# Gate projections of a hybrid decoder layer, done in pairs by seven half-size products

## The chip, the cores and the metric

The kernel runs on one core of a Trainium2 chip. The metric is device time in microseconds (us); smaller is better. Times are those of whole executions, with a profile of one execution beside them. Engines: TensorE (PE, matmul), VectorE (DVE), ScalarE (ACT), GpSimd (POOL) and SyncE (SP, which issues most DMAs).

## The reference

One layer in float32, 512 tokens of 2048 channels. The input is RMS-normalised and projected by `w_in`; one branch is a gated linear recurrence (HGRN2, 8 heads), the other sparse attention (NSA, 16 heads in 4 groups: compressed, selected and window keys). Both go through an output matrix, are merged by sigmoid gates, and go through `w_out` with a residual and a last norm. What matters here:

```
xn = rmsnorm(h, norm_w[layer])
proj = xn @ w_in[layer]                      # 2048 x 15408, the last 4096 columns are merge_g
o_hg = hgrn2_chunkwise(...) ; y_hg = o_hg @ w_branch_hg[layer]
o_nsa = nsa_attention(...) * silu(nsa_z)     # nsa_z: 2048 columns of proj
y_nsa = o_nsa @ w_branch_nsa[layer]
g_hg, g_nsa = split(sigmoid(merge_g))
h = h + (g_hg * y_hg + g_nsa * y_nsa) @ w_out[layer]
return rmsnorm(h, final_norm_w)
```

## The kernel before

All products are done in float32r with both operands split in a high and a low part: high x high, high x low, low x high (`mm3`, L133 to L136). The weights come from HBM in units of 512 KB (`load_w`, L111): SP issues the load into one of three buffers `wr`, ACT casts it to the high part `wh` (L125), DVE subtracts to get the low part `wl` (L126); `wh` and `wl` have two buffers each. `split` (L129) does the same for other tiles. A projection of 128 columns (`proj_units`, L138) takes two units and 16 steps, one per row block; a step is three matmuls of 512 columns (all tokens). It gives back control after each step, so that `weave` (L170) can lay the steps of another generator between them, with two numbers that say how many steps each has.

The stages, in order: the ramp (L190: normalise, transpose x to `xh` and `xl`, first values and branch gates, token tile by token tile); HGRN2 (L305: `hg_proj` of the next head woven with `hg_core` of this one; every second `hg_proj` also does a pair of values by `proj_v`, 64 steps of three 256-column matmuls); NSA compression (L497); the four NSA groups (L566: `nsa_proj` of the next group woven with `nsa_core`, 220 steps against 48); the branch outputs and merge (L745); the output projection (L776).

The 32 gate tiles (`merge_gates`, L159: a projection, Sigmoid on ACT, a DMA by POOL to `gat_d` in DRAM) are filler. Three lie beside the last HGRN2 core (L474), 16 in the compression (L509), 8 beside the last NSA core (L741), 5 in the wait for the branch inputs (L748). The 16 z tiles are in `nsa_proj` (`z_proj`, L586), 64 of its 220 steps; they are multiplied into the attention output at L723 and L734. The HGRN2 branch output is computed in the last loop (L767) beside the NSA one.

The framework sets each engine's order by priorities, in general that of the code; `tc.high_priority()` puts a unit's split ahead.

Of the kernel before, what the change touches and what calls it, by code (L numbers as in the profile page):

```python
# [8 lines left out]
F32 = mybir.dt.float32  # L9
# [9 lines left out]
KD = D // P  # L19
HG = 8  # L20
# [25 lines left out]
def constants():  # L46
    """Tables that depend on shapes alone: identity, causal masks, RoPE angles, block masks."""
# [27 lines left out]
def body(tc, a, out):  # L75
# [33 lines left out]
    gat_d = dram.tile([2, KD, P, S], F32, name="gat_d")  # L109

    def load_w(src, k0, nk, *cols, raw=None, hi=None, lo=None, urgent=True):  # L111
        """A unit of weights (nk row blocks, the given column ranges) and its exact split in two float32r parts."""
# [25 lines left out]
    def proj_units(acc, src, c0, ncol, xh, xl, nk):  # L138
        """acc[ncol, tokens] = src[:, c0:c0+ncol]^T x, in steps of one row block."""
# [7 lines left out]
    def proj_v(vb, cols):  # L147
        """vb[i // 2][tokens, i % 2, 256 columns] = x w_in[:, cols], two token tiles to a bank."""
# [17 lines left out]

    def proj_t(*args):
# [15 lines left out]
    xh = xpool.tile([P, KD, S], F32R, name="xh")  # L183
    xl = xpool.tile([P, KD, S], F32R, name="xl")
# [5 lines left out]
    with pool("st_a") as sp:  # L190
        xt = [sp.tile([P, D], F32, name="xt", bufs=4) for _ in range(4)]
# [14 lines left out]
        # the activation table and the tensor engine's clock are up by the time the data arrives  # L206
# [98 lines left out]
    with pool("hg") as hp:  # L305
        hgw = sv[:, R_HGW:R_HGW + 1]
        heads = {}
        vts = {0: vt}
# [3 lines left out]
        def hg_proj(head):  # L312
            pr, e = divmod(head, 2)
            if pr and not e:
                vb = [bank() for _ in range(2)]
                yield from proj_v(vb, ((C_HI + pr * 256, 256),))
                v = vts[pr] = vpool.tile([P, 4, 2, P], F32, name="vt", bufs=2)
                for n in range(2):
                    nc.scalar.copy(v[:, 2 * n:2 * n + 2].rearrange("p j e c -> p (j e c)"), vb[n])
# [15 lines left out]
        def hg_core(head):  # L335
# [136 lines left out]
        for head in range(HG - 1):  # L472
            weave(hg_proj(head + 1), 112 if head % 2 else 48, hg_core(head), 17)
# [23 lines left out]
    with pool("cp") as cp:  # L497
# [14 lines left out]
        for b, (w1, w2, pos0, b0) in enumerate(((a["cmp_k_w1"], a["cmp_k_w2"], R_KP, R_KB),  # L512
# [5 lines left out]
            for l0 in range(0, CLEN, 8):  # L518
# [344 lines left out]
```

## Time and profile before

| | us |
|---|---|
| three executions | 2112.49, 2110.85, 2112.24 (median 2112.24) |
| span of the profiled execution | 2108.8 |
| PE, DVE, ACT, POOL busy in it | 2085.3, 998.1, 746.6, 310.6 |

Of the profiled execution the span is given, from the first to the last instruction; what lies around it is not in it. Busy times of PE are modelled: a matmul's duration contains its way through the array, which overlaps with the next, so the time that a matmul costs is read from how many start in a stretch. In the views a line is that of the code, tiles are written out<-in, and `[... <-X]` tells what ended the idle time ahead of an instruction.

### The profile page before, as it was taken

Reading aid. Unit: us, or ns where it says so; the run is one execution under the profiler, and the core shown is the slowest. Engines: PE = TensorE matmul, PEld = TensorE weight load, DVE = VectorE, ACT = ScalarE, POOL = GpSimd, SP = SyncE. Lnnn points to the kernel's source line nnn. Section 1 sums busy time; section 2 is a strip of 40 time slices with the busy share of each in tenths; the row PEclk is TensorE's granted clock in tenths of the full one; section 3 lists DMA queues with packets and bytes.
Section 4 is the critical chain, followed back from the end, with each engine's and each line's share of the span. In section 5 each row is a group of like instructions: output and inputs, shape, how many; then the busy total and the mean of one; then the engine's idle time right before and its main releaser. Section 6 shows DMA issues by size and latency. Waiting matters only on the chain.

```text
span 2108.8 us, 26626 instructions
## 1 busy us (share of the span) xinstructions
PE 2085.3 (99%) x10560; PEld 1761.7 (84%) x10560; DVE 998.1 (47%) x1595; ACT 746.6 (35%) x1149; POOL 310.6 (15%) x367
## 2 busy tenths in 40 slices
PE   8999999999999999999999999999999999999998
PEld 7888888888888888889889888888888888888887
DVE  7364636365544432435545555555553433433343
ACT  4223232333233433225344444434553322222232
POOL 2131414132000000101311221121220000000000
PEclk9999999999999999999999999999999999999999
DMA  6223222234355554332222232223225744445232
GB/s 184 61 85 86 83 82 80 81 85 115 100 158 171 171 171 120 100 96 70 77 81 81 78 84 80 75 74 89 79 83 169 209 130 123 127 133 201 95 132 88
DMA packets 328641, 231.38 MB, mean 110 GB/s; under 512 B 9931, under 2 KB 298516, under 8 KB 327876
## 3 DMA queue, kind: packets, MB, share of 16 engines
q1 hardware_dynamic: 316388, 198.36, 32.5%
q10 hardware_dynamic: 7552, 16.57, 2.1%
q0 software_dynamic: 4576, 14.75, 2.1%
q8 instruction: 83, 1.36, 0.3%
q14 instruction: 42, 0.34, 0.1%
HBM read 210.71 MB, written 18.94 MB: 109 GB/s over the span
## 4 chain that ended last, share of the span: by engine, by line
PE 93%; DVE 3%; issue 2%; POOL 1%; ACT 1%; DMA 0%; SPq 0%; DVEq 0%; POOLq 0%; ACTq 0%
PE pj L134 23%; PE pj L136 23%; PE pj L135 23%; PE sc L135 4%; PE sc L134 4%; PE sc L136 4%; PE pt L708 2%; PE po L134 2%; PE po L135 2%; PE po L136 2%; DVE wl L126 1%; PE pt L396 1%; PE pt L136 1%; PE pt L134 1%; PE pt L135 1%
## 5 line engine op out<-in xcount | busy, mean ns | idle before, releaser
L126 DVE TENSOR_TENSOR wl<-wr,wh 128x1024 fp32r<-128x1024 f32 x308 | 382.1, 1241 | 609.4 <-ACT wh L125 606.2
L134 PE MATMUL pj<-xh,wh 128*128 128x512 f32 x1664 | 659.0, 396 | 0.0
L136 PE MATMUL pj<-xh,wl 128*128 128x512 f32 x1664 | 651.7, 392 | 0.4 <-DVE wl L126 0.4
L135 PE MATMUL pj<-xl,wh 128*128 128x512 f32 x1664 | 649.2, 390 | 0.0
L125 ACT CAST wh<-wr 128x1024 fp32r<-128x1024 f32 x308 | 323.5, 1051 | 845.6 <-PE pj L135 610.6
L136 PEld LDWEIGHTS pj<-xh,wl 128*128 128x128 f32 x1664 | 312.4, 188 | 68.0 <-DVE wl L126 1.2
L134 PEld LDWEIGHTS pj<-xh,wh 128*128 128x128 f32 x1664 | 312.7, 188 | 61.3 <-DVE vl L131 0.6
L135 PEld LDWEIGHTS pj<-xl,wh 128*128 128x128 f32 x1664 | 312.8, 188 | 60.4
L134 PE MATMUL pj<-wh,xh 128*128 128x256 f32 (+1 forms) x544 | 167.0, 307 | 0.0
L136 PE MATMUL pj<-wh,xl 128*128 128x256 f32 (+1 forms) x544 | 164.0, 301 | 0.0
L135 PE MATMUL pj<-wl,xh 128*128 128x256 f32 (+1 forms) x544 | 163.9, 301 | 0.0
L689 POOL TENSOR_SCALAR s<-s,sm 128x512 f32<-128x512 f32 (+3 forms) x128 | 87.7, 697 | 192.8 <-DVE sm L687 112.8
L135 PEld LDWEIGHTS pj<-wl,xh 128*128 128x128 f32 x544 | 103.6, 190 | 4.7
L134 PEld LDWEIGHTS pj<-wh,xh 128*128 128x128 f32 x544 | 103.5, 190 | 4.8
L136 PEld LDWEIGHTS pj<-wh,xl 128*128 128x128 f32 x544 | 103.5, 190 | 3.8
L134 PE MATMUL pj<-onh,wh 128*128 128x512 f32 x256 | 99.6, 389 | 0.0
L135 PE MATMUL pj<-onl,wh 128*128 128x512 f32 x256 | 99.6, 389 | 0.0
L136 PE MATMUL pj<-onh,wl 128*128 128x512 f32 x256 | 99.6, 389 | 0.0
L684 ACT ACTIVATE s<-s,mx 128x512 f32<-128x512 f32 (+3 forms) x128 | 70.9, 555 | 58.7 <-DVE mx L682 57.6
L131 DVE TENSOR_TENSOR ptl<-pt,pth 128x512 fp32r<-128x512 f32 (+1 forms) x80 | 50.7, 634 | 77.1 <-ACT pth L130 77.0
L493 POOL TENSOR_TENSOR rsh<-rsh,rope 32x512 f32<-32x512 f32 x28 | 45.5, 1626 | 240.5 <-DVE rsh L492 224.6
L361 POOL TENSOR_TENSOR suf<-suf,pre 128x256 f32<-128x256 f32 x56 | 57.3, 1022 | 124.1 <-DVE pre L344 105.1
(316 smaller groups left out, 2715.4 us busy)
## 6 DMA issues: line engine op xcount, KB each, us to landing
wr<-in_w_in_dram SPq DMA_DIRECT2D x220, 512.0 KB, 3.7
wr<-in_w_branch_nsa_dram SPq DMA_DIRECT2D x32, 512.0 KB, 3.9
wr<-in_w_out_dram SPq DMA_DIRECT2D x32, 512.0 KB, 3.7
wr<-in_cmp_k_w_dram SPq DMA_DIRECT2D x16, 512.0 KB, 3.5
wr<-in_cmp_v_w_dram SPq DMA_DIRECT2D x16, 512.0 KB, 3.6
wr<-in_w_in_dram SPq DMA_DIRECT2D x32, 256.0 KB, 3.4
gg<-gat_d ACTq DMA_DIRECT2D x16, 512.0 KB, 4.3
wr<-in_w_branch_hg_dram SPq DMA_DIRECT2D x16, 512.0 KB
```

The lines of the kernel that those rows point to most:

```text
L125: nc.scalar.copy(hi[:, :n], raw[:, :n])
L126: nc.vector.tensor_tensor(lo[:, :n], raw[:, :n], hi[:, :n].bitcast(F32), op=OP.subtract)
L131: nc.vector.tensor_tensor(lo, src, hi.bitcast(F32), op=OP.subtract)
L134: nc.tensor.matmul(acc, lhsT=lh, rhs=rh, start=start, stop=False, **kw)
L135: nc.tensor.matmul(acc, lhsT=lh, rhs=rl, start=False, stop=False, **kw)
L136: nc.tensor.matmul(acc, lhsT=ll, rhs=rh, start=False, stop=stop, **kw)
L361: nc.gpsimd.tensor_tensor(fv[:, :, 0], fv[:, :, 0], whole(pv[:, :, 1]), op=OP.mult)
L396: nc.tensor.matmul(pv[:, j].rearrange("p (m h) -> p m h", h=h), lhsT=qk[:, j * P:(j + 1) * P], rhs=up, start=True, stop=True)
L493: nc.gpsimd.tensor_tensor(sh, sh, sin, op=OP.mult)
L684: nc.scalar.activation(s[:, b], s[:, b], AF.Exp, scale=SCALE, bias=mx[:, b:b + 1], accum_out=sm[:, b:b + 1])
L689: nc.gpsimd.tensor_scalar(s[:, b], s[:, b], sm[:, b:b + 1], 1.0, op0=OP.mult, op1=OP.mult)
L708: nc.tensor.transpose(ps[:, o:o + P], sc[i][:, b, j * P:(j + 1) * P], ident)
```

## The change

Twenty-six of the 32 gate tiles are computed between the ramp and HGRN2, in 13 pairs. A pair is a product of 256 columns of `w_in`, 2048 rows and 512 tokens; each of the three is halved, and in place of eight products of halves there are seven, with sums of halves of x (made once, `sums`, with 64 transposes) and sums of halves of the weights (made on DVE for every pair). A half-size product (`product`) has eight row blocks: the high weights are loaded and 512 columns stream by (256 tokens of the high and 256 of the low part of x), then the low weights with the 256 columns of the high part. The two halves of a bank are added later on DVE.

The values of the second pair of heads are done with `sums`, ahead of the pairs; the z tiles and the HGRN2 branch output become filler (`z_units`, `y_hg`, through `z_d` and `part_d` in DRAM), six gate tiles stay as filler ahead of the branch stage, and z is multiplied in when the attention output is read back.

```diff
+NG = 26
+    def z_units(n0, n1, pl, tag="mg"):
+        for n in range(n0, n1):
+            acc = bank()
+            yield from proj_units(acc, w_in, C_Z + n * DH, DH, xh, xl, KD)
+            st = pl.tile([P, S], F32, name=tag, bufs=2)
+            nc.scalar.activation(st, acc, AF.Sigmoid)
+            nc.vector.tensor_tensor(st, acc, st, op=OP.mult)
+            nc.gpsimd.dma_start(z_d[n], st)
+    def sevens(src, c_lo, c_hi, kh, side, chain, keeps, done):
...
+        def load(r, c0, dst=None):
+            if dst is None:
+                dst = wp.tile([P, 1024], F32, name="wr", bufs=3)
+            nc.sync.dma_start(v(dst), block(r, c0))
+            return dst
+        def add(dst, r, c0):
+            more = load(r, c0)
+            with tc.high_priority():
+                nc.vector.tensor_tensor(dst[:, :kh * P], dst[:, :kh * P], more[:, :kh * P], op=OP.add)
+        def parts(raw):
+            hi, lo = (wp.tile([P, 1024], F32R, name=n, bufs=2) for n in ("wh", "wl"))
+            with tc.high_priority():
+                split(hi[:, :kh * P], lo[:, :kh * P], raw[:, :kh * P])
+            return v(hi), v(lo)
+        def product(acc, p, w, first):
+            av = acc.rearrange("p (b t) -> p b t", b=2)
+            for k in range(kh):
+                x = side(p, k)
+                nc.tensor.matmul(av, lhsT=w[0][:, k], rhs=x, start=first and k == 0, stop=False, skip_group_check=True)
+                nc.tensor.matmul(av[:, 0], lhsT=w[1][:, k], rhs=x[:, 0], start=False, stop=k == kh - 1,
+                                 skip_group_check=True)
...
+        load(0, c_lo, X)
+        A = bank()
+        w = parts(X)
+        add(X, 0, c_hi)
+        load(0, c_hi, Y)
+        yield from product(A, 0, w, True)
+        nc.scalar.copy(s1, A)
+        B = bank()
+        w = parts(X)
+        add(Y, 1, c_hi)
+        add(X, 1, c_hi)
+        yield from product(B, 1, w, True)
+        nc.scalar.copy(s5, B)
+        b22 = load(1, c_hi)
+        w, w2 = parts(X), parts(b22)
+        add(X, 1, c_lo)
+        yield from product(A, 2, w, False)
+        nc.scalar.copy(s2, A)
+        yield from product(B, 3, w2, False)
+        nc.vector.tensor_tensor(s2, B, s2, op=OP.add)
+        yield from product(A, 4, parts(Y), False)
+        nc.vector.tensor_tensor(s5, A, s5, op=OP.add)
+        b21 = load(1, c_lo)
+        B = bank()
+        yield from product(B, 5, parts(b21), True)
+        nc.vector.tensor_tensor(s2[:, :h], s2[:, :h], s2[:, h:], op=OP.add)
+        nc.vector.tensor_tensor(s2[:, h:], s5[:, :h], s5[:, h:], op=OP.add)
+        nc.vector.tensor_tensor(s1, B, s1, op=OP.add)
+        nc.vector.tensor_tensor(s1[:, :h], s1[:, :h], s1[:, h:], op=OP.add)
+        yield from product(A, 6, parts(X), False)
+        nc.scalar.copy(s5[:, :h], A[:, h:])
+        nc.vector.tensor_tensor(s1[:, h:], A[:, :h], s5[:, :h], op=OP.add)
+        done(s1, s2)
...
+        def sums():
...
+            for n, (i0, c0) in enumerate(((2, H), (0, 0), (0, H), (2, 0))):
+                for t in range(2):
+                    for k0 in (0, 4):
+                        ps = lbank().rearrange("p (k t) -> p k t", k=4)
+                        for k in range(4):
+                            c = c0 + (k0 + k) * P
+                            nc.tensor.transpose(ps[:, k], xt[i0 + t][:, c:c + P], ident)
+                        ts = slice(t * P, (t + 1) * P)
+                        split(sx[:, 0, n, k0:k0 + 4, ts], sx[:, 1, n, k0:k0 + 4, ts], ps)
+                        yield
+        weave(values(1), 64, sums(), 16)
...
+            def gates(lo, hi):
+                for o, v, sign in ((0, lo, 1.0), (1, hi, -1.0)):
+                    nc.scalar.activation(v, v, AF.Sigmoid, scale=sign)
+                    nc.gpsimd.dma_start(gat_d[(n + o) // KD, (n + o) % KD], v)
...
-            weave(hg_proj(head + 1), 112 if head % 2 else 48, hg_core(head), 17)
-        weave(merge_gates(0, 3, hp), 48, hg_core(HG - 1), 17)
+            weave(hg_proj(head + 1), 112 if head in (3, 5) else 48, hg_core(head), 17)
+        weave(z_units(0, 3, hp), 48, hg_core(HG - 1), 17)
...
-        fill = merge_gates(3, 19, cp)
+        def y_hg():
+            for c in range(KD):
+                acc = bank()
+                yield from proj_units(acc, a["w_branch_hg"], c * P, P, og[0], og[1], HG)
+                g = cp.tile([P, S], F32, name="mg", bufs=2)
+                nc.scalar.dma_start(g, gat_d[0, c])
+                nc.vector.tensor_tensor(g, acc, g, op=OP.mult)
+                nc.gpsimd.dma_start(part_d[c], g)
+        def both():
+            yield from z_units(3, 8, cp)
+            yield from y_hg()
+        fill = both()
...
-                    for _ in range(8):
+                    for _ in range(6 + l // 2 % 2):
...
-        weave(nsa_proj(g + 1), 220, nsa_core(g), 48)
-    weave(merge_gates(19, 27, ap, "raw"), 112, nsa_core(GROUPS - 1), 48)
+        weave(nsa_proj(g + 1), 156, nsa_core(g), 48)
+    weave(z_units(8, 16, ap, "raw"), 112, nsa_core(GROUPS - 1), 48)
...
-        fill = merge_gates(27, 32, bp)
+        fill = merge_gates(NG, 32, bp)
```

Behind the ramp DVE's row before is that of HGRN2's first heads: splits of weight units (`wl`), with the core's work behind them.

```order
L126 TENSOR_TENSOR wl<-wr,wh 128x1024 x4
L332 TENSOR_TENSOR zs<-pj,zs 128x512
L126 TENSOR_TENSOR wl<-wr,wh 128x1024 x2
L342 TENSOR_SCALAR kt<-sg,nomlb,omlb 128x512
L344 TENSOR_SCALAR pre<-sg,omlb,lbt 128x512
```

Now one pair stands there 13 times. Below is DVE from the first split of a pair (its first buffer is `xt_2155`, the next pair's is `xt_2333`, loaded operands are `wr`, `xt_908` and `s2` hold results; L134 is a split, L203 an add of weights).

```order
L134 TENSOR_TENSOR wl_2160<-xt_2155,wh_2159 128x1024
L203 TENSOR_TENSOR xt_2155<-xt_2155,wr_2163 128x1024
L252 TENSOR_TENSOR xt_908<-pj_1980,xt_908 128x256
L134 TENSOR_TENSOR wl_2186<-xt_2155,wh_2185 128x1024
L203 TENSOR_TENSOR xt_2155<-xt_2155,wr_2192 128x1024
L134 TENSOR_TENSOR wl_2215<-xt_2155,wh_2214 128x1024
L203 TENSOR_TENSOR xt_2155<-xt_2155,wr_2222 128x1024
L134 TENSOR_TENSOR wl_2219<-wr_2212,wh_2218 128x1024
L134 TENSOR_TENSOR wl_2260<-xt_2155,wh_2259 128x1024
L240 TENSOR_TENSOR s2_2156<-pj_2184,s2_2156 128x512
L203 TENSOR_TENSOR xt_2333<-xt_2333,wr_2367 128x1024
L134 TENSOR_TENSOR wl_2284<-wr_2280,wh_2283 128x1024
```

Between two splits of the same buffer stands the add that changes it; the split of the sixth product (the last row) stands behind a sum that reads the fourth product's bank and behind the first add of the next pair.

On ACT the row before, in HGRN2, is casts of weight units (`wh`) between the core's copies and activations.

```order
L125 CAST wh<-wr 128x1024
L330 ACTIVATE zs<-pj 128x512
L432 COPY kn<-pt 128x384
L441 COPY st<-sc 128x128
L455 ACTIVATE ob<-po 128x512
```

Now ACT has this across the end of a pair (`xt_2333` is the pair's first buffer, `xt_2511` that of the next; L451 is a gate's Sigmoid).

```order
L133 CAST wh_2461<-wr_2458 128x1024
L133 CAST wh_2485<-xt_2333 128x1024
L451 ACTIVATE s2_2334<-s2_2334 128x512
L133 CAST wh_2515<-xt_2511 128x1024
L251 COPY xt_908<-pj_2336 128x256
L133 CAST wh_2541<-xt_2511 128x1024
```

The Sigmoid of a gate stands ahead of the first cast of the next pair, and a copy out of the seventh product's bank ahead of the second.

SP issues the eight loads of a pair in one row. Six of them share the three buffers `wr`, so each waits until DVE has done with an earlier one: the load for the first add of the next pair waits for the third add of this one, and the load behind it, for the add to `Y` of the next pair, for the split of the fourth product.

## Rows read from the trace of the kernel before

**Rows 1.** The page: busy time of the engines, and the chain that ended last.
```profile
PE 2085.3 (99%) x10560; PEld 1761.7 (84%) x10560; DVE 998.1 (47%) x1595; ACT 746.6 (35%) x1149; POOL 310.6 (15%) x367
...
PE 93%; DVE 3%; issue 2%; POOL 1%; ACT 1%; DMA 0%; SPq 0%; DVEq 0%; POOLq 0%; ACTq 0%
```

**Rows 2.** Busy time in stretches of the span (first row: the columns).
```profile
core 0: us, PE busy (x) PEld busy (x) DVE busy (x) ACT busy (x) POOL busy (x), PEclk, DMA share, GB/s
0.00:61.00 61.00, 51.19 (x286) 45.30 (x287) 40.35 (x65) 28.48 (x47) 13.99 (x14) 0.92 0.52 159
61.00:503.00 442.00, 438.13 (x2562) 374.81 (x2561) 229.30 (x318) 133.30 (x182) 126.63 (x137) 1.00 0.29 82
503.00:819.00 316.00, 315.55 (x1407) 259.41 (x1407) 137.29 (x120) 116.64 (x134) 16.64 (x22) 1.00 0.53 154
820.00:839.00 19.00, 19.00 (x161) 19.00 (x160) 3.68 (x3) 3.14 (x3) 0.58 (x1) 1.00 0.29 78
...
1481.00:1592.00 111.00, 110.58 (x554) 92.09 (x553) 58.77 (x163) 61.98 (x124) 24.58 (x41) 1.00 0.28 79
1592.00:1700.00 108.00, 108.00 (x477) 89.03 (x476) 45.61 (x43) 37.49 (x42) 5.07 (x9) 1.00 0.62 187
1700.00:1850.00 150.00, 150.00 (x663) 124.23 (x662) 57.99 (x65) 35.13 (x37) 0.00 (x0) 1.00 0.44 133
```

**Rows 3.** Waits of PE over the span: total us, times, longest us.
```profile
PE sc L396 <- DVE ad L400: 3.9, 7, 0.8
...
PE pj L136 <- DVE wl L126: 0.4, 1, 0.4
PE po L134 <- ACT pch L130: 0.4, 1, 0.4
```

**Rows 4.** Groups by line and shape: count | busy us, mean ns | idle before.
```profile
L126 DVE TENSOR_TENSOR wl<-wr,wh 128x1024 fp32r<-128x1024 f32 x308 | 382.1, 1241 | 609.4 <-ACT wh L125 606.2 <-DMA wr<-in_w_in_dram 3.0
L125 ACT CAST wh<-wr 128x1024 fp32r<-128x1024 f32 x308 | 323.5, 1051 | 845.6 <-PE pj L135 610.6 <-PE pj L136 68.0 <-PE po L136 51.7
...
L362 DVE TENSOR_TENSOR pre<-pre 128x256 f32<-128x256 f32 x56 | 26.7, 477 | 15.5 <-POOL suf L361 15.2
...
L164 ACT ACTIVATE mg<-pj 128x512 f32<-128x512 f32 x24 | 14.2, 592 | 0.0
...
L772 DVE TENSOR_TENSOR gg<-gg 128x512 f32<-128x512 f32 x16 | 11.1, 692 | 0.5
```

**Rows 5.** PE in order of time: four transposes and the next product.
```profile
1065.91 0.60 PE L708 MATMUL pt<-ident,s 128*128 128x128 f32 x4
1066.27 0.43 PE L134 MATMUL po<-pth,vh 128*128 128x384 f32 x1
```

**Rows 6.** Timeline (start, us): two DVE instructions; release, cast, split; a late product.
```profile
42.24 1.22 DVE L126 TENSOR_TENSOR wl<-wr,wh 128x1024 fp32r<-128x1024 f32 x1
43.38 0.68 DVE L131 TENSOR_TENSOR xl<-pt,xh 128x512 fp32r<-128x512 f32 x1
...
303.69 0.39 PE L135 MATMUL pj<-xl,wh 128*128 128x512 f32 x1
...
304.12 1.05 ACT L125 CAST wh<-wr 128x1024 fp32r<-128x1024 f32 x1 [0.95 <-PE pj L135]
...
305.20 1.22 DVE L126 TENSOR_TENSOR wl<-wr,wh 128x1024 fp32r<-128x1024 f32 x1 [1.32 <-ACT wh L125]
...
567.69 0.50 PE L136 MATMUL pj<-xh,wl 128*128 128x512 f32 x1 [0.45 <-DVE wl L126]
```

**Rows 7.** The chain in order of time (start, us): the split ahead of that last product.
```profile
566.50 1.14 DVE wl L126
```

**Rows 8.** DMA issues: count, KB each, median us from issue to landing.
```profile
wr<-in_w_in_dram SPq DMA_DIRECT2D x220, 512.0 KB, 3.7
...
xt<-in_x_dram SPq DMA_DIRECT2D x8, 512.0 KB, 5.4
```

More of the change, by code (lines that the diff above doesn't have):

```diff
@@ L109, in body @@
     gat_d = dram.tile([2, KD, P, S], F32, name="gat_d")
+    part_d = dram.tile([KD, P, S], F32, name="part_d")
+    z_d = dram.tile([GROUPS * HPG, P, S], F32, name="z_d")
     def load_w(src, k0, nk, *cols, raw=None, hi=None, lo=None, urgent=True):
@@ L187, in body @@
     vpool = hgp.enter_context(pool("hgv"))
+    xtp = ExitStack()
+    xtpool = xtp.enter_context(pool("xt"))
+    xt = [xtpool.tile([P, D], F32, name="xt", bufs=4) for _ in range(4)]
     with pool("st_a") as sp:
-        xt = [sp.tile([P, D], F32, name="xt", bufs=4) for _ in range(4)]
         wu = []
@@ L305, in body @@
+    xtp.close()
     with pool("hg") as hp:
@@ L313, in hg_proj @@
             pr, e = divmod(head, 2)
[L314 to L319, printed above, removed]
+            if pr > 1 and not e:
+                yield from values(pr)
             pq = bank()
@@ L508, in body @@
                     nc.scalar.copy(raw[:, g], acc)
-        fill = merge_gates(3, 19, cp)
+        og = [cp.tile([P, HG, S], F32R, name=n) for n in ("ogh", "ogl")]
+        for h in range(0, HG, 2):
+            raw = wp.tile([P, 1024], F32, name="wr", bufs=3)
+            nc.sync.dma_start(raw.rearrange("p (h s) -> p h s", h=2), ohg_d[h:h + 2].rearrange("h p s -> p h s"))
+            f = lambda t: t[:, h:h + 2].rearrange("p h s -> p (h s)")
+            split(f(og[0]), f(og[1]), raw)
+        def y_hg():
[10 more added lines that the diff above has]
+        fill = both()
         for b in range(2):
@@ L583, in nsa_proj @@
             q.append((qh, ql))
-        z = {}
-        def z_proj(h):
-            acc = bank()
-            yield from proj_units(acc, w_in, C_Z + (g * HPG + h) * DH, DH, xh, xl, KD)
-            z[h] = ap.tile([P, 384], F32, name="zs", bufs=3)
-            for d, c in ((z[h], slice(0, 384)), (z3[:, h], slice(384, S))):
-                nc.scalar.activation(d, acc[:, c], AF.Sigmoid)
-                nc.vector.tensor_tensor(d, acc[:, c], d, op=OP.mult)
-        z3 = ap.tile([P, HPG, P], F32, name="z3", bufs=2)
-        for h in range(3):
-            yield from z_proj(h)
         kh = ap.tile([P, 2, S], F32R, name="kh", bufs=1)
@@ L604, in nsa_proj @@
             split(kh[:, b], kl[:, b], raw)
-        groups[g] = vh, vl, q, z, kh, kl, z3
-        yield from z_proj(3)
+        groups[g] = vh, vl, q, kh, kl
     def nsa_core(g):
-        vh, vl, q, z, kh, kl, z3 = groups[g]
+        vh, vl, q, kh, kl = groups[g]
         vcz = [ap.tile([P, HPG, DH], F32R, name=n) for n in ("vczh", "vczl")]
@@ L749, in body @@
         for _ in range(20):
             next(fill)
-        for src, dst, nh in ((ohg_d, og, HG), (ons_d, on, 16)):
-            for h in range(0, nh, 2):
-                raw = wp.tile([P, 1024], F32, name="wr", bufs=3)
-                nc.sync.dma_start(raw.rearrange("p (h s) -> p h s", h=2), src[h:h + 2].rearrange("h p s -> p h s"))
-                f = lambda t: t[:, h:h + 2].rearrange("p h s -> p (h s)")
-                split(f(dst[0]), f(dst[1]), raw)
-                for _ in range(5):
-                    next(fill, None)
+        for h in range(0, 16, 2):
+            raw, zr = (bp.tile([P, 1024], F32, name=n, bufs=3) for n in ("raw", "zr"))
+            for d, src in ((raw, ons_d), (zr, z_d)):
+                nc.sync.dma_start(d.rearrange("p (h s) -> p h s", h=2), src[h:h + 2].rearrange("h p s -> p h s"))
+            nc.vector.tensor_tensor(raw, raw, zr, op=OP.mult)
+            f = lambda t: t[:, h:h + 2].rearrange("p h s -> p (h s)")
+            split(f(on[0]), f(on[1]), raw)
+            for _ in range(8):
+                next(fill, None)
```

72 lines of the change are left out of this document (55 added, 17 removed).

## The prediction

> **What bounds the kernel now.** I read the page's busy times first, then the chain that ended last, then the busy time by stage, and last what the tensor engine (PE) waited for. PE is busy 99% of the span and makes 93% of the chain; VectorE (DVE) is busy less than half of the time [rows 1]. By stage the reader is to see one thing: the matmuls follow each other without a gap. In the branch stage 663 products of 512 columns fill 150 us, 0.2265 us each (the ends of the window cut one or two); in a stretch of value projections 161 products of 256 columns fill 19 us, 0.1195 us each without the two cut ones [rows 2]. So half the columns take a little more than half the time, the weight load does not stand in the way, and the granted clock is at its upper level (1.00, 2.4 GHz). Behind the ramp PE's named waits are 3.9 us at L396, and 0.4 us each at two other places [rows 3]. The work that feeds PE has slack: a weight unit is a cast on ScalarE (ACT) of 1.05 us and a subtraction on DVE of 1.24 us [rows 4], for eight steps of three products, 5.4 us. What the change takes from PE is therefore worth its full time, as long as the new stage keeps PE as busy as the old stages did.
>
> **What is removed and added on PE.** A gate tile is 16 steps of three 512-column products, 48; 26 of them are 1248, at 0.2265 us 282.7 us. In their place stand 13 pairs of seven products of eight row blocks, each a 512-column and a 256-column matmul: 728 of each, at 0.2265 + 0.1195 = 0.346 us, 251.9 us. One product is 8 x 0.346 = 2.77 us, a pair 19.4 us where it was 21.7. The 64 transposes of the sums of x are 16 groups of four; a group takes 0.36 us to the next product [rows 5], with the wait for its bank 0.4, so 6.4 us. Net: -282.7 + 251.9 + 6.4 = -24.4 us, if nothing waits.
>
> The Trainium skill, "TensorE: Matmul & The Clock Gate", section "Back-to-back issue gap", puts a warm product at N/2.4 + 2.5 ns, 109 ns for 256 columns and 216 for 512. The trace does not agree, it has 119.5 and 226.5. By the page the products would give back 269.3 - 236.6 = 32.7 us in place of 30.8, 2 us more.
>
> **What the pairs wait for.** This stage has no filler: the products of a pair stand behind each other, and every one needs its own split. On DVE a pair has seven splits and four sums of 1024 columns (1.24 us, the sum by the row of the same shape), three sums of 512 (0.69) and four of 256 (0.48): 17.6 us of 19.4 [rows 4]. That fits in total, so what decides is the order. The first buffer of a pair is used four times, each time changed in place: cast, split, add, cast, split, add. Handing over costs about 0.03 us from ACT to DVE, and the cast starts 0.43 us after the start of the last product that reads its buffer [rows 6]. The second matmul of a product needs the low part, and follows the end of the split by 0.05 us (split from 566.50 to 567.64, product L136 at 567.69) [rows 6, 7].
>
> Let t = 0 be the start of the seventh product of the pair before. The high buffer is free at 0.1, but on ACT the Sigmoid of the last gate (0.59 us) stands ahead of the cast, and waits for DVE's sums: I put the cast at 0.45. Cast to 1.50, split to 2.77, add to 4.04, cast to 5.12, split to 6.39, second matmul at 6.44. PE gets there after two products and one matmul, at 2 x 2.77 + 0.23 = 5.77: a wait of 0.7 us in the second product. Then add to 7.66, cast to 8.74, split to 10.01, matmul at 10.06; PE would be there 2.77 after 6.44, at 9.21: a wait of 0.85 us in the third. The fourth and fifth products have their operands in other buffers and do not wait. In the sixth, DVE first does the 512-column sum behind the fourth product and the first add of the next pair (1.24), and only then the split: some 0.3 us late by itself. That add needs a load which SP may issue only when the split of the fourth product has freed a buffer, some 1.1 us after another load of 512 KB. A load lands 3.7 us after its issue [rows 8]; at full rate it occupies the DMA engines for 1.85 us (0.29 busy at 82 GB/s gives 283 GB/s [rows 2]), so the second of two lands some 0.7 us later than alone. I take 0.6 us for the sixth product.
>
> Together 2.15 us per pair, 21.5 us in place of 19.4, and 13 x 2.15 = 28.0 us. The bounds: DVE starts an instruction 0.08 us before the one ahead has ended (1.22 at 42.24, the next at 43.38 [rows 6]); if that holds along the whole chain, and the load is in time, 0.85 us is left, 11 us in all. Loads that all land 1.5 us later make it some 3 us, 39 in all.
>
> The loads themselves fit: eight of 512 KB and two writes of 256 KB in 21.5 us are 219 GB/s, against the 283 of above.
>
> **The rest.** The eight sums of x, 1.24 us each, go to DVE while it is busy 40 of the ramp's 61 us [rows 2]; three stand ahead of the last splits of x, for which PE waits: 0.5 us, between 0 and 3. Value projections of the second pair of heads move ahead of HGRN2; they cost PE the same there. The core of head 1 then has 48 filler steps in place of 112; PE's wait at L396 is 3.9 us in seven cores, the longest 0.8 [rows 3], so I add 0.5, between 0 and 2. In the three woven NSA groups 64 of 220 filler steps go. How a core does with little filler is shown by the last group: 112 steps, 111 us, PE busy 110.58 [rows 2]. Three times the missing 0.4 is 1.2 us, between 0 and 8. The z tiles and the HGRN2 branch output that now fill the compression are the same products at another place; their Sigmoids, multiplications and transfers lie beside PE (DVE 137, ACT 117 of 316 us there [rows 2]) and cost nothing unless a split is late behind them: 0 to 3, I take 0.
>
> **Sum.** -24.4 + 28.0 + 0.5 + 0.5 + 1.2 = +5.8 us on the span of 2108.8, 2114.6. The profiled execution's time is given as its span alone; the median of the runs, 2112.2, lies 3.4 us above it, so I forecast 2118.0 us, +0.27%.
>
> **Rivals.** *Faster: the chain is shorter than its listed durations.* For it speaks the 0.08 us overlap, and that DVE has 10% left. Against it, each step needs the data of the step ahead, and a step that waits for such data started 0.03 us behind its end [rows 6]. With 1.0 us per pair in place of 2.15 it gives 2118 - 15 = 2103. It decides from 1.4 us per pair: 2118 - 13 x 0.75 = 2108, 0.2% below before.
>
> *No change.* One of the waits is off (the load comes in time, or the Sigmoid is not in the cast's way): 1.4 to 2.0 us per pair, 2108 to 2116, middle 2112.
>
> *Slower, by late loads.* Eight loads per 21.5 us where it was four per 21.7, three shared buffers, and SP issues in order. For it: four times in a pair a load is issued only when DVE has finished with a buffer. Against it: the densest stretch behind the ramp, 187 GB/s, kept PE busy for all of its 108 us [rows 2], if with fewer short rows. In the ramp loads of x took 5.4 us [rows 8], some of it behind each other; half way, 4.6 in place of 3.7, puts 0.9 us more on the sixth product, 12 us: 2130. The Trainium skill, "DMA: Bandwidth & Descriptors", section "Latency and other measured facts", says that HBM access takes 0.2 us on average and 2 us under high load. By that rule a load at this traffic would take up to 5.5 us, and the stage 13 x 1.8 = 23 us more, 2141; no row has 219 GB/s of loads in 512-byte rows for long, and the 3.7 us are a median over stretches of 82 to 187 GB/s.
>
> *Slower, by the thinner weave.* If the NSA cores need more than 156 steps, each group waits some 3 us: 2126. The last group speaks against it.
>
> **Chances.** Forecast (waits of 2.0 to 2.6 us per pair, 2116.5 to 2124) 0.33; faster 0.27; no change 0.25; late loads 0.11; thin weave 0.04. A measurement of this kernel can tell 0.2% (4.2 us) from no change; so faster than 2108.0 is 0.27, within 0.25, above 2116.5 is 0.48. Leaving 0.1 out at each end, the range goes from 2102 (waits of 0.9) to 2132 (late loads); the forecast's own is 2116 to 2124.
>
> **What would show it.** Right: in the stage behind the ramp some 21.5 us per pair, PE's waits at the second matmul of a product (L216) of 0.7, 0.85 and 0.6 us for DVE's split, in the second, third and sixth product, and 0.346 us per row block. The first two waits would still be there if all loads came early; the third would show DVE waiting for a DMA in an add (L203). Wrong: pairs of 20.3 us or less, waits at the first matmul (L215), which would mean casts or banks, loads landing over 5 us after issue, or new PE waits in the NSA groups above 1 us.

## The result, and the profile after

The changed kernel takes 2138.3 us (median of four runs, 2136.4 to 2138.7) where the kernel before takes 2112.0: a ratio of 1.0124 (95 % interval 1.0109 to 1.0138), 26 us slower. Forecast were 2118.0 us and a range up to 2132. The direction was right, the size was not.

The page of the changed kernel, the lines that answer to [rows 1]:

```profile
PE 2076.8 (97%) x10832; PEld 1756.8 (82%) x10832; DVE 1168.2 (55%) x1789; ACT 791.3 (37%) x1219; POOL 321.9 (15%) x399
...
PE 74%; DVE 11%; DMA 5%; ACT 4%; issue 3%; POOL 2%; SPq 0%; DVEq 0%; ACTq 0%; POOLq 0%
```

PE is busy for 8.5 us less, in a span that is 28.1 us longer (2136.9), and its share of the chain falls from 93 % to 74 %. DVE, loads and ACT have come into the chain: the new time is waiting, not work. The stages answer to [rows 2] (same columns): ramp, pairs, HGRN2 (two rows), the three woven NSA groups, last group, branch stage:

```profile
0.00:61.00 61.00, 49.11 (x289) 44.31 (x290) 48.87 (x64) 27.09 (x45) 14.63 (x14) 0.92 0.50 159
...
90.00:377.00 287.00, 263.80 (x1456) 222.10 (x1456) 213.75 (x233) 135.50 (x170) 13.89 (x25) 1.00 0.76 208
377.00:503.00 126.00, 125.19 (x644) 103.48 (x643) 63.40 (x89) 37.91 (x52) 34.44 (x40) 1.00 0.31 88
503.00:806.00 303.00, 299.33 (x1770) 255.61 (x1770) 165.63 (x234) 95.21 (x131) 92.75 (x99) 1.00 0.28 83
...
1168.00:1576.00 408.00, 401.51 (x2233) 347.99 (x2233) 244.89 (x601) 174.89 (x381) 100.35 (x132) 1.00 0.25 71
1576.00:1694.00 118.00, 116.94 (x582) 97.28 (x580) 66.79 (x176) 62.42 (x125) 26.75 (x42) 1.00 0.28 82
1694.00:1830.00 136.00, 134.58 (x591) 110.28 (x590) 57.69 (x56) 39.85 (x46) 5.64 (x10) 1.00 0.62 195
```

In the kernel before, the three groups are this row, with no idle time of PE:

```profile
948.50:1481.00 532.50, 532.50 (x2827) 458.16 (x2826) 289.20 (x652) 231.25 (x446) 107.44 (x132) 1.00 0.29 80
```

In the pairs PE is idle for 23 of 287 us, in the NSA groups for 6.5 of 408, and the granted clock is at its upper level (1.00) in both. PE's waits say for what (total us, times, longest); only the HGRN2 one, the second line, was there before [rows 3]:

```profile
PE pj L216 <- DVE wl L134: 23.2, 36, 2.4
PE sc L546 <- DVE ad L550: 4.5, 7, 0.8
...
PE po L138 <- DVE ptl L134: 3.6, 3, 1.3
...
PE sc L137 <- DVE mx L837: 2.4, 6, 0.6
```

All waits in the pairs stand at L216, the second matmul, as forecast, none at L215. What each stage loses can be added up, in both kernels, from the time between the start of one matmul and the start of the next: what it is above 0.2265 us (512 columns) or 0.1195 us (256) is lateness. By term, in us, with the forecast:

| term | forecast | measured |
|---|---|---|
| products, at the durations of before | -30.8 | -30.8 |
| transposes of the sums of x | +6.4 | +7.0 |
| pairs, second product (13 times) | +9.1 | +6.6 |
| pairs, third product | +11.1 | +10.9 |
| pairs, sixth product | +7.8 | +15.6 |
| pairs, pace of a row block (0.349 us, not 0.346) and the rest | 0 | +2.4 |
| ramp and HGRN2 | +1.0 | +1.1 |
| compression | 0 | -0.4 |
| three NSA groups | +1.2 | +11.5 |
| last NSA group and branch stage | 0 | +1.5 |
| last matmul to the end of the span | 0 | +2.6 |
| sum (of unrounded terms) | +5.8 | +28.1 |

**The sixth product.** Its wait is 1.1 to 1.5 us in most pairs, where 0.6 was forecast. DVE in one pair (start, us; what ended the idle time ahead):

```profile
207.13 1.22 DVE L134 TENSOR_TENSOR wl<-wr,wh 128x1024 fp32r<-128x1024 f32 x1
209.83 1.23 DVE L134 TENSOR_TENSOR wl<-xt,wh 128x1024 fp32r<-128x1024 f32 x1 [1.49 <-ACT wh L133]
211.69 0.69 DVE L240 TENSOR_TENSOR s<-pj,s 128x512 f32<-128x512 f32 x1 [0.64 <-PE pj L216]
213.45 1.23 DVE L203 TENSOR_TENSOR xt<-xt,wr 128x1024 f32<-128x1024 f32 x1 [1.06 <-DMA wr<-in_w_in_dram]
214.59 1.22 DVE L134 TENSOR_TENSOR wl<-wr,wh 128x1024 fp32r<-128x1024 f32 x1
```

The first row is the split of the fourth product's weights. It frees the buffer into which SP then issues the load for the sum that DVE does first for the next pair (the one into `Y`), 1.13 us behind another load:

```profile
207.24 0.37 SPq L197 DMA_DIRECT2D wr<-in_w_in_dram  x1
...
208.37 0.37 SPq L197 DMA_DIRECT2D wr<-in_w_in_dram  x1
```

DVE comes to that sum (L203) at 212.38 and has nothing to add until 213.45: the load took 5.1 us. The split that PE needs for the sixth product, whose high part is ready since 212.57, is behind it in DVE's queue. DVE's waits for these loads in the stage (total us, times, longest), and the loads into `wr` (count, KB, median us to landing):

```profile
DVE xt L203 <- DMA wr<-in_w_in_dram: 11.0, 12, 2.2
```

```profile
wr<-in_w_in_dram SPq DMA_DIRECT2D x76, 512.0 KB, 4.9
```

4.9 us stands where [rows 8] has 3.7. But the trace resolves the landing of only 13 of these 76 loads; ten of them were issued 3.5 to 5 us behind the load ahead, and the late one above is not among them. So its 5.1 us rests on the rows above, not on this median.

**The NSA groups.** The longest wait, once per group, in order of time:

```profile
1245.32 0.68 DVE L644 TENSOR_TENSOR raw<-raw,rope 32x512 f32<-32x512 f32 x1
...
1245.44 1.72 POOL L643 TENSOR_TENSOR rsh<-rsh,rope 32x512 f32<-32x512 f32 x1 [0.96 <-DVE rsh L642]
...
1247.01 0.36 PE L137 MATMUL po<-pth,vh 128*128 128x256 f32 x1
1247.19 0.68 DVE L645 TENSOR_TENSOR raw<-raw,rsh 32x512 f32<-32x512 f32 x1 [1.18 <-POOL rsh L643]
1247.80 0.67 DVE L134 TENSOR_TENSOR ptl<-pt,pth 128x512 fp32r<-128x512 f32 x1
...
1248.52 0.39 PE L138 MATMUL po<-ptl,vh 128*128 128x256 f32 x1 [1.15 <-DVE ptl L134]
```

In the rotation of a head, POOL multiplies by the sines for 1.72 us. DVE comes to the last sum (L645) and stands for 1.18 us; the split of the probabilities, which has nothing to do with the rotation and whose operand ACT has had ready since 1245.47, stands behind it, and PE waits. The Trainium skill, "Perfetto Trace Analysis", section "Tensor Engine Instruction (MATMUL, LD_WEIGHTS)", says that DVE, ACT and GpSimd are strictly first in, first out; these rows agree: the split starts at 1247.80, behind the sum that starts at 1247.19.

**The end.** From the last matmul to the end of the span it is 8.9 us before and 11.5 after. The longest of the DRAINs on POOL's queue (an instruction at the end of the program; min/median/max in ns) ends last; before:

```profile
L853 POOLq DRAIN  x3: 46/102/6372, 2101.6 to 2108.5; - x3
```

and after:

```profile
L1007 POOLq DRAIN  x3: 46/102/8989, 2127.1 to 2136.6; - x3
```

POOL issues 61 DMAs before, 93 after.

**The branch stage.** Two loads of 512 KB per step stand where one did, and the weights of the gate tiles stand behind them. The chain that ended last (start, us; its longest pieces) goes through such a load:

```profile
1733.94 9.90 DMA zr<-z_d
1743.93 1.24 DVE raw L910
1747.41 1.23 DVE wl L129
```

### The profile page after: what moved, and what is told of

It is laid out like the page before. It is cut to its first block, busy times and chain, and to the rows that moved or that the text cites. A ratio compares the mean times of both kernels' runs of the same rounds, so it can differ in the third digit from the quotient of the medians.

```text
span 2136.9 us, 27863 instructions
## 1 busy us (share of the span) xinstructions
PE 2076.8 (97%) x10832; PEld 1756.8 (82%) x10832; DVE 1168.2 (55%) x1789; ACT 791.3 (37%) x1219; POOL 321.9 (15%) x399
## 4 chain that ended last, share of the span: by engine, by line
PE 74%; DVE 11%; DMA 5%; ACT 4%; issue 3%; POOL 2%; SPq 0%; DVEq 0%; ACTq 0%; POOLq 0%
PE pj L137 19%; PE pj L139 19%; PE pj L138 18%; DVE wl L134 4%; DMA wr<-in_w_in_dram 3%; PE sc L137 2%; PE sc L138 2%; PE sc L139 2%; ACT wh L133 2%; DVE wl L129 2%; PE po L138 2%; DVE xt L203 2%; PE pt L865 1%; PE po L139 1%; PE po L137 1%
## 5 line engine op out<-in xcount | busy, mean ns | idle before, releaser
L137 PE MATMUL pj<-xhl,wh 128*128 128x512 f32 x1248 | 497.0, 398 | 0.7 <-ACT wh L128 0.7
L139 PE MATMUL pj<-xhl,wl 128*128 128x512 f32 x1248 | 489.8, 392 | 0.7 <-DVE wl L129 0.7
L138 PE MATMUL pj<-xhl,wh 128*128 128x512 f32 x1248 | 487.4, 391 | 0.0
L139 PEld LDWEIGHTS pj<-xhl,wl 128*128 128x128 f32 x1248 | 234.3, 188 | 52.4 <-DVE wl L129 2.2
L137 PEld LDWEIGHTS pj<-xhl,wh 128*128 128x128 f32 x1248 | 234.6, 188 | 45.4 <-ACT wh L128 1.1
L138 PEld LDWEIGHTS pj<-xhl,wh 128*128 128x128 f32 x1248 | 234.7, 188 | 44.4
L137 PE MATMUL pj<-wh,xhl 128*128 128x256 f32 (+1 forms) x544 | 168.0, 309 | 0.0
L138 PE MATMUL pj<-wl,xhl 128*128 128x256 f32 (+1 forms) x544 | 164.0, 302 | 0.0
L139 PE MATMUL pj<-wh,xhl 128*128 128x256 f32 (+1 forms) x544 | 164.0, 302 | 0.0
L215 PE MATMUL pj<-sx,wh 128*128 128x512 f32 x416 | 147.0, 394 | 0.0
L216 PE MATMUL pj<-sx,wl 128*128 128x256 f32 x416 | 119.2, 287 | 10.6 <-DVE wl L134 10.6
L215 PE MATMUL pj<-xhl,wh 128*128 128x512 f32 x312 | 110.2, 394 | 0.0
L137 PEld LDWEIGHTS pj<-wh,xhl 128*128 128x128 f32 x544 | 103.4, 190 | 5.2
L138 PEld LDWEIGHTS pj<-wl,xhl 128*128 128x128 f32 x544 | 103.5, 190 | 4.9
L139 PEld LDWEIGHTS pj<-wh,xhl 128*128 128x128 f32 x544 | 103.3, 190 | 3.9
L134 DVE TENSOR_TENSOR wl<-xt,wh 128x1024 fp32r<-128x1024 f32 x65 | 79.6, 1224 | 46.5 <-ACT wh L133 46.5
L216 PE MATMUL pj<-xhl,wl 128*128 128x256 f32 x312 | 88.7, 284 | 12.6 <-DVE wl L134 12.6
```

Of the source, the lines that this page charges most:

```text
L134: nc.vector.tensor_tensor(lo, src, hi.bitcast(F32), op=OP.subtract)
L137: nc.tensor.matmul(acc, lhsT=lh, rhs=rh, start=start, stop=False, **kw)
L138: nc.tensor.matmul(acc, lhsT=lh, rhs=rl, start=False, stop=False, **kw)
L139: nc.tensor.matmul(acc, lhsT=ll, rhs=rh, start=False, stop=stop, **kw)
L215: nc.tensor.matmul(av, lhsT=w[0][:, k], rhs=x, start=first and k == 0, stop=False, skip_group_check=True)
L216: nc.tensor.matmul(av[:, 0], lhsT=w[1][:, k], rhs=x[:, 0], start=False, stop=k == kh - 1, skip_group_check=True)
```

## The experiments

Each time is a median of 4 to 12 runs, with the ratio to runs of the kernel before on the same chip beside it. Edits are to the changed kernel unless said otherwise.

**Writes issued by ACT**

```diff
-            nc.gpsimd.dma_start(...)        # in all eight places
+            nc.scalar.dma_start(...)
```

> All writes to the DRAM tiles that GpSimd (POOL) issued, 93 of them, are issued by ScalarE (ACT) instead. Theory: POOL's DRAIN at the end of the program lasts in proportion to the DMAs that POOL has issued (6.37 us with 61 before, 8.99 us with 93 after, 0.082 us each), so with none it falls to some 1.4 us; the end is then set by the last output write, and the stretch from the last matmul to the end goes from 11.5 to 7.7 us: 2134.5 us. Rival 1: the DRAIN is of fixed length or depends on something else (the last loads): 2138. Rival 2: ACT stands behind writes whose data DVE has not yet made, its casts come late, and PE waits more than is won: 2140 to 2150.

2137.1 us, ratio 1.0125 [1.0111, 1.0139]. The DRAIN fell to what was expected:

```profile
L1007 POOLq DRAIN  x3: 40/82/1383, 2129.0 to 2134.8; - x3
```

The stretch behind the last matmul fell from 11.5 to 7.8 us, 3.7 as expected. But the last matmul itself came 1.9 us later. The branch stage lost 1 us more than in the changed kernel, and one sixth product came 3.6 us late: PE waited 1.9 us in it, and behind that wait the granted clock stood at its lower level (0.50, 1.2 GHz) for 3.4 us:

```profile
307.00:310.40 3.40, 3.40 (x13) 2.92 (x12) 1.43 (x2) 0.77 (x2) 0.00 (x0) 0.50 1.06 284
```

So the DRAIN is as long as its count of DMAs says, and the time of this edit alone can't be told from that of the changed kernel: the intervals overlap.

**Sums without loads**

```diff
-            more = load(r, c0)
+            more = dst
```

> The four sums of weights in a pair add the buffer to itself, and their four loads of 512 KB are left out (the gates are then other numbers); every DVE and ACT instruction stays. Theory A (PE's wait in the sixth product, 1.33 us per pair, comes from the load that the first sum of the next pair needs, and which lands 5 us after it is issued): that wait falls to 0.3 us or less, the waits in the second and third products (0.55, 0.86) stay, a pair takes 21.0 us in place of 22.2: 2138 - 14 = 2124. Rival B (the sixth split is late because DVE has the sum and the add ahead of it, whenever the load comes): the wait stays at 1.1 to 1.3 us, 2136 to 2138. Rival C (all loads of the stage are late and all waits come of that): 0.3 us per pair is left, 2112.

2151.0 us, 1.0185 [1.0171, 1.0199]: none of the three. The sixth product's wait did go (0.04 us), as theory A had it, but the second product took 2 to 6 us longer in ten pairs. With the loads gone, the framework puts another sum, of the buffer Y, ahead of the split of the second product, and that sum waits for the load of Y (third row; the split behind it is the fourth):

```profile
207.00 1.23 DVE L203 TENSOR_TENSOR xt<-xt 128x1024 f32<-128x1024 f32 x1
208.15 0.42 DVE L252 TENSOR_TENSOR xt<-pj,xt 128x256 f32<-128x256 f32 x1
210.57 1.23 DVE L203 TENSOR_TENSOR xt<-xt 128x1024 f32<-128x1024 f32 x1 [2.01 <-DMA xt<-in_w_in_dram]
211.71 1.22 DVE L134 TENSOR_TENSOR wl<-xt,wh 128x1024 fp32r<-128x1024 f32 x1
```

PE's waits in the stage are 28.7 us, the longest 3.5. The clock took more: between these waits the granted clock fell to its lower level (0.50, 1.2 GHz) six times, for 23.8 us in all, where it stayed at 1.00 in the changed kernel. At half the clock, and less what PE waited in them, these stretches cost some 10 us, an estimate. Over the stage and in the longest of these stretches:

```profile
90.00:391.00 301.00, 272.33 (x1471) 232.68 (x1471) 217.62 (x236) 137.72 (x172) 13.82 (x25) 0.96 0.39 108
187.10:193.90 6.80, 5.89 (x18) 5.06 (x19) 4.53 (x4) 2.00 (x3) 0.00 (x0) 0.50 0.00 0
```

So the edit changed three things, and its time tells nothing about the load alone; it shows a sum's wait for a load ahead of a split at another place.

**No sums**

```diff
-            more = load(r, c0)
-            with tc.high_priority():
-                nc.vector.tensor_tensor(dst..., dst..., more..., op=OP.add)
+            load(r, c0)
```

> The four sums in a pair are left out, their loads stay (products of the first buffer then use the unsummed weights). Theory A: the chain cast, split, add, cast, split of the first buffer is what makes the second and third products wait, and the add that waits for its load what makes the sixth wait; all three waits vanish, a pair takes 19.6 to 20.0 us: 2138 - 13 x 2.4 = 2107. Rival D (the DMA engines, busy 76 % of the stage, cannot deliver eight loads and two writes in less than 22 us): the waits move to other products, casts wait for loads, a pair stays above 21.5 us: 2130 or more.

2108.8 us, 0.9987 [0.9978, 0.9995]. No wait in the pairs is left; PE's busy time in the stage, and the DMA share, 0.84:

```profile
90.00:347.00 257.00, 257.00 (x1457) 222.90 (x1457) 156.21 (x182) 134.11 (x170) 13.83 (x25) 1.00 0.84 224
```

A pair takes 19.79 us, 29.5 us less in all. All eight loads and both writes fit into that, so it is the sums, and what stands ahead of and behind them, that make the three waits (33 us), not the amount of data (rival D falls).

**Filled pairs**

```diff
+        more = z_units(0, 3, mp, u=4, bufs=1, pb="po")   # units of 4 steps
...
-            for _ in sevens(...):
-                pass
+            for i, _ in enumerate(sevens(...)):
+                if n and i == 3:
+                    for _ in range(4):
+                        next(more, None)
```

> Three z tiles (48 steps) that filled the core of the last HGRN2 head are done in units of four steps behind the first product of pairs 2 to 13, the fills behind move up (the compression gets 5 steps per unit in place of 6.5). The work of PE is the same in sum. Theory A (the pairs wait because nothing stands between their products while DVE goes through the first buffer's chain): 2.7 us of other products behind the first one cover the waits in the second and third products, and the sixth has had time too: 2.3 of the 2.7 us per pair vanish, 2138 - 12 x 2.3 = 2110. Rival (DVE, 17.6 us of work in a pair of 19.4, or the loads are the bound, and the added split and load push the waits back by as much): 2130 to 2138. Rival: the compression, with fewer steps, waits for its own loads: 5 us of the gain are lost there.

2120.1 us, 1.0041 [1.0029, 1.0054]: 18 us back, of 28 expected. The second and sixth waits are gone, the third is 0.58 us still, and 0.25 to 1.1 us arose at a new place, the second matmul of the first product. DVE does the sum into `Y` first, which in the second pair waits 0.73 us for its load, and then the split that PE needs:

```profile
108.12 1.23 DVE L203 TENSOR_TENSOR xt<-xt,wr 128x1024 f32<-128x1024 f32 x1 [0.73 <-DMA wr<-in_w_in_dram]
109.27 1.22 DVE L134 TENSOR_TENSOR wl<-xt,wh 128x1024 fp32r<-128x1024 f32 x1
...
110.54 0.39 PE L216 MATMUL pj<-xhl,wl 128*128 128x256 f32 x1 [0.88 <-DVE wl L134]
```

The filler itself does not wait. The first rival, that the work on DVE pushes the waits elsewhere, is right in part. DVE's waits for loads at L203, 1.7 us where they were 11.0:

```profile
DVE xt L203 <- DMA wr<-in_w_in_dram: 1.7, 4, 0.7
```

**A buffer for the fourth product**

```diff
-        b22 = load(1, c_hi)
+        b22 = load(1, c_hi, mp.tile([P, 1024], F32, name="wq"))
```

> The weights of the fourth product get a buffer of their own, so that the three shared ones go round among the loads of the sums and of the sixth product; the load for the first sum of the next pair then need not wait for the split of the fourth product. The work is the same. Theory A (PE's wait in the sixth product, 1.33 us per pair, is that load landing late): the wait falls to 0.4 us or less, those in the second and third products stay at 0.5 and 0.85: 2138.3 - 12 = 2126. Rival B (the split of the sixth product is late because the sum of 512 columns and the add stand ahead of it on DVE): the wait stays above 1 us, 2137. Rival D (an earlier load only makes the others later, since all eight share the DMA engines): the wait moves to the second or the seventh product, 2135 to 2145.

2123.9 us, 1.0055 [1.0043, 1.0068]: 14.4 us less, theory A. The sixth wait is 0.04 us in 11 of 12 pairs, the second and third stay at 0.40 to 0.55 and 0.84 to 0.91. PE's waits, and the landing of the loads into `wr` and into the first buffers:

```profile
PE pj L216 <- DVE wl L134: 9.6, 21, 0.6
```

```profile
wr<-in_w_in_dram SPq DMA_DIRECT2D x63, 512.0 KB, 3.8
xt<-in_w_in_dram SPq DMA_DIRECT2D x23, 512.0 KB, 5.8
```

The traffic is 219 GB/s, higher than the 208 of before this edit. The two medians are of few loads (2 into `wr`, 11 into `xt`), so I count the DMA packets in the trace, 1024 of 512 bytes to a load, in order of issue. From the issue to the end of a load's last packet it takes 3.2 us here if the load ahead was issued 3.5 us or more before (median of 49), 4.4 if it was 1.1 us before (12), and 5.0 if it was 0.4 us before (13); landings that the trace resolves come 0.4 us or more later. In HGRN2 of the kernel before, at 82 GB/s, with no loads closer than 3.5 us, it is 3.15 us (53). So a load is late because of the one issued right ahead of it, not because of the mean traffic; the edit gives the place close behind another load to the fourth product's, and the sum finds its load landed. The Trainium skill ("DMA: Bandwidth & Descriptors", "Latency and other measured facts") gives 2 us of HBM access under high load in place of 0.2. Between 82 and 219 GB/s that does not show in loads that stand apart.

**The rotation on DVE**

```diff
-        nc.gpsimd.tensor_tensor(sh, sh, sin, op=OP.mult)
+        nc.vector.tensor_tensor(sh, sh, sin, op=OP.mult)
```

> In the rotation of a head (L643) the multiplication by the sines is done by DVE in place of POOL. Theory: once per NSA group PE waits 1.4 to 1.6 us in a product of probabilities and values (L137 to L138 of po), because DVE stands at the rotation's last sum (L645), waiting 1.2 us for POOL (1.72 us), with the split of the probabilities behind it; DVE itself needs 0.69 us, so the three waits fall from 4.3 us in sum to 2 or less, and the time to 2135.5. Rival: the weave is too thin as such, the wait comes back at the next place: 2138. Rival: DVE's 28 more instructions of 0.69 us (19 us over the program) push back other splits: 2140.

2130.7 us, 1.0089 [1.0075, 1.0102]: 7.6 us less, more than the one wait per group that I had put it on. All NSA waits listed for PE are gone but for one of 0.3 us; PE is busy for 407.4 of 408 us:

```profile
1165.00:1573.00 408.00, 407.36 (x2270) 354.29 (x2269) 255.19 (x627) 176.90 (x384) 72.26 (x114) 1.00 0.27 73
```

From the first transposes of `pc` in the first core (L784; L627 before) to those in the fourth it is 399.9 us, where the changed kernel has 408.9: 9.1 less. The kernel before has 527.9 there, of which 130.5 are the 12 z tiles that have gone elsewhere; so 2.4 of the 11.5 us more are left.

**The weave counted by length**

```diff
-                    yield                                    # proj_v of nsa_proj
+                    if not halves or i % 2:
+                        yield
...
-        weave(nsa_proj(g + 1), 156, nsa_core(g), 48)
+        weave(nsa_proj(g + 1), 124, nsa_core(g), 48)
```

> In the three NSA groups the 64 steps of value projections, which are half as long as the others (three products of 256 columns, 0.36 us, in place of 0.68), count in pairs: 124 steps in place of 156 against the 48 of the core. Theory: the waits at the start of each group (0.77 and 0.35 us at the scores, 0.3 to 0.5 behind) are there because a step of the core then has 3.25 x 0.36 = 1.17 us of other products beside it, against 1.65 in the kernel before (4.58 x 0.36) and 1.59 in its last group; counted by length it has 2.58 x 0.72 = 1.9 us, and some 1.4 us per group vanish: 2134. Rival: behind the value projections the cover falls from 2.2 to 1.8 us per step of the core, and new waits of that size arise there: 2138 or more.

2140.0 us, 1.0136 [1.0120, 1.0151]: the rival. The waits at the scores went; others of the same size came, and that behind the rotation stayed:

```profile
PE pt L785 <- ACT pc L781: 3.9, 4, 1.1
PE po L138 <- DVE ptl L134: 3.3, 3, 1.1
```

My theory of the half-length steps falls: evening out the cover moves PE's waits and does not remove them.

**The kernel before, with the rotation on DVE** (the edit as above)

> The kernel before, with the multiplication by the sines (L493) done by DVE in place of POOL. Theory (the detour over POOL cost nothing before, since 4.58 steps of other products per step of the core covered it, and became a wait only with 3.25 steps): no change, 2110.5 to 2112.5. Rival (the detour cost the same in both kernels, so the 7.6 us that the same edit gave in the changed kernel are no part of the difference between the two): 2104 to 2106.

2111.9 us, 1.0000 [0.9992, 1.0009]: no change. In the trace of before DVE waits for POOL at L495 just as long as after at L645, and PE does not notice (total us and times over the span, before and after):

```profile
  POOL rsh L493: 22.4, 19
...
  POOL rsh L643: 22.8, 22
```

So the detour costs nothing in one kernel and 7.6 us in the other. What differs beside it is the filler, 156 steps where there were 220; that the thinner weave is the reason is argued from this, as no run puts the steps back.

**Three edits**: the own buffer, the rotation on DVE, and gates and z tiles written by ACT.

> The changed kernel with three edits: the own buffer for the fourth product's weights, the rotation's multiplication on DVE, and the 48 writes of gates and z tiles issued by ACT (45 stay on POOL, so its DRAIN should last 1.4 + 45 x 0.082 = 5.1 us and end before the last output write has landed). Theory: the three causes are separate and add up: 2138.3 - 14.4 - 7.6 - 3.7 = 2112.6. Rival: the writes on ACT (0.35 us each, two per pair, behind the Sigmoids) push back the casts of the first buffer, and the waits in the second and third products grow by 0.3 to 0.5 us: 2117 to 2122.

2110.0 us, 0.9996 [0.9987, 1.0004]: the three add up; the 2.6 us beyond them lie within the interval. The 3.7 among them is what the stretch at the end fell by; the time of that run alone fell by 1.2. The DRAIN with 45 DMAs on POOL, 5.1 us expected:

```profile
L1007 POOLq DRAIN  x3: 46/93/5066, 2102.1 to 2107.8; - x3
```

**Filled pairs, rotation, ACT's writes**

```diff
+        more = z_units(0, 3, mp, bufs=1, pb="po", u=2, own=own)   # own ur, uh, ul of 1 KB
...
+                if n and i in (3, 7):
+                    for _ in range(2):
+                        next(more, None)
```

> The changed kernel with the rotation on DVE, the 48 writes from ACT, and three z tiles done between the products of pairs 2 to 13 in units of two steps with buffers of their own: two steps behind the first product, two behind the second (the own buffer for the fourth product does not fit beside them). The fills behind move up as in the run with filled pairs. Theory: the three waits of a pair are covered (0.55 by the first 1.36 us, 0.86 by the second, the sixth has had 2.7 us more), a pair takes 19.8 + 2.7 us: 2138.3 - 13 x 2.4 - 7.6 - 3.7 = 2096. Rival: the 24 small loads stand in SP's order between those of the pair, make them later, and waits of 0.5 us or more per pair stay: 2103 to 2110.

2107.7 us, 0.9984 [0.9975, 0.9992], runs from 2103.6 to 2112.6. The second and third waits are gone (0.02 us), the sixth is 0.1 to 1.6 us: with the small loads in SP's queue the sum's load is late again, and not by the same amount in each pair. DVE's waits for it:

```profile
DVE xt L203 <- DMA wr<-in_w_in_dram: 12.6, 12, 1.8
```

The rival. That this is also why the runs differ by 9 us is a guess; one run was traced.

**The same, with a buffer for the fourth and sixth products**

```diff
+        extra = xtpool.tile([P, 2, 1024], F32, name="xt", bufs=4)
-        b22 = load(1, c_hi)
+        b22 = load(1, c_hi, extra[:, 0])
-        b21 = load(1, c_lo)
+        b21 = load(1, c_lo, extra[:, 1])
```

> As the run with filled pairs, rotation on DVE and ACT's writes, and in it the weights of the fourth and sixth products get an 8 KB buffer of their own, taken from the four of the first buffers (which then are loaded one pair ahead in place of two). Theory: the sixth product's wait (0.1 to 1.6 us, with the load for the next pair's first sum late again) goes, a pair takes 22.6 us in place of 23.1, and runs differ less from each other: 2096 to 2098, some 0.7 % below the kernel before. Rival: the first buffers' loads, now one pair ahead, come late at the first product: 2104 or more.

2098.7 us, 0.9938 [0.9925, 0.9952]. From the third pair on every pair takes 22.20 us, of which 2.72 are the four steps of filler: 19.48 for seven products, the 19.4 of the sum. Runs go from 2096.1 to 2102.3. PE in the stage:

```profile
90.00:377.00 287.00, 286.74 (x1602) 249.59 (x1601) 226.88 (x259) 147.69 (x196) 0.00 (x0) 1.00 0.83 222
```

**And wider steps in the branch stage**

```diff
-        for _ in range(20):                 # 20 -> 12 steps ahead, 8 -> 10 between
+        for _ in range(12):
```

> As the run before, and in the branch stage the eight steps that load, multiply and split the outputs have ten steps of gate products between them in place of eight (and twelve ahead of the first in place of twenty). Theory: PE's three waits in that stage (2.2 us more than in the kernel before) come from weights that stand in SP's queue behind the two loads of 512 KB per step, where there was one; with 25 % more time per step they fall by 1 us or more: 1 to 2 us below the run before. Rival: the loads of the last core's outputs wait for its writes anyway and hold SP's queue, whatever stands between: the same as the run before, or 1 us more.

2096.0 us, 0.9926 [0.9913, 0.9938], 0.74 % faster than the kernel before. It can't be told from the run ahead of it: the intervals overlap, and the lateness in that stage is no smaller (0.5 us more in the traced runs). What would remove it stays open.

## Why the prediction was wrong

What held: the products give back what the matmuls' intervals say; the waits stand at the second matmul, in the products named, for DVE's splits; the third product's wait is 0.86 us where 0.85 was worked out, the second's 0.55 where it was 0.7. That the sums make them, the run without sums shows.

**The sixth product's term was mis-sized.** The step "the second of two lands some 0.7 us later than alone. I take 0.6 us for the sixth product" had the right parts, an add ahead of the split and a load issued 1.1 us behind another one. The load took 5.1 us in place of 4.4, and the wait is 1.2 us per pair on average (15.6 in sum; none in the first pair and the last). The rival of late loads had this very place and 0.9 us more on it; measured are 0.6. The own buffer took the wait away for 14.4 us. Why two loads took longer than the 3.7 us and 283 GB/s of the rows give is not shown.

**The step on the thinner weave failed.** "How a core does with little filler is shown by the last group" took a stretch as a model that lacks the work that matters: beside the last group there are only gate tiles, no heads that are rotated. DVE's wait for POOL was in the trace of before and cost nothing there, with 220 steps beside it (the edit changed nothing in that kernel); with 156 it cost 7.6 us. That rival was given 9 us, close to the measured 10 above the forecast, and a chance of 0.04. By the edit, the detour is 7.6 us of the time, and 9.1 of the 11.5 in the traced runs; the 2.4 left are not traced further.

**Two terms were missing.** The end of the program was put at nothing; of the new transfers the prediction says only that they "lie beside PE". POOL's DRAIN grew by 2.6 us with the 32 more DMAs, as the three other counts (0, 45, 61) bear out. The branch stage has twice the loads, and some 2 us of new waits; that these come from SP's queue is read from the chain and was not confirmed by the one run on it.

The rivals were weighed as if one of them would happen. Late loads and the thinner weave came together, each with about its price: on the span, 2114.6 + 7.5 (pairs) + 10.3 (groups) + 2.6 (end) and + 1.9 in the stages between is 2136.9 (the median lies 1.4 us above the span here, where 3.4 was taken: each run's time lies 1.7 to 2.0 us above its own span, and 3.4 set a median against the span of a faster run). Their sum lay outside the range because the range was drawn over cases that exclude each other. The 2141 that the prediction works out for loads under load lies near the measured time by luck: the pairs are 7.5 us above the forecast, not 23, and loads that stand apart took no longer.

## What to carry to other kernels

Where filler is taken out of a stage, look for the waits that the filler hides now: each place where an engine's queue stands for a slower engine or a load with another's work behind it is a cost in waiting, and a stretch serves as a model only if it holds the same work. A sum that needs a load belongs behind the splits that PE waits for (not run here), or its buffer must be freed by something early, as with the own buffer. When independent stages each lose cover, add their prices in the range.

## What was new of the hardware

POOL's DRAIN at the end of the program lasts longer the more DMAs POOL has issued: 1.38, 5.07, 6.37 and 8.99 us with 0, 45, 61 and 93, 0.082 us each. The same multiplication of 32 x 512 elements takes 1.71 us on POOL (median of 28) and 0.68 on DVE. Beside POOL's multiplication, DVE's product of that shape takes 1.02 us on average in the kernel before (L494), and 0.67 once POOL no longer does it. Loads of 512 KB in 512-byte rows have their last packet 3.2 us after the issue at 219 GB/s and 3.15 at 82, if no other was issued in the 3.5 us ahead; 1.1 us behind another load it is 4.4, in the run with the own buffer.
